# Order of the splits at two seams and width of the last product in a one-core decoder layer

## The chip, the cores and the metric

The kernel runs on one core of one Trainium2 chip. The metric is the device time of one execution in microseconds; lower is better.

## The reference

One layer of a decoder over 256 tokens of 1024 features, in float32: half a feed-forward network (SwiGLU, 2816 wide), a mixer (block attention of 8 heads beside a causal pooling mixer), cross-attention to 256 memory tokens, and half a feed-forward network again. Each sub-layer normalises its input, and normalises its output before it is added to the stream:

```python
def rmsnorm(x, g):
    r = lax.rsqrt(jnp.mean(x * x, axis=-1, keepdims=True) + RMS_EPS)
    return (x * r) * g

h = rmsnorm(x, ffn1_pre_g);  x = x + 0.5 * rmsnorm(swiglu(h, w_gate, w_up, w_down), ffn1_post_g)
h = rmsnorm(x, mix_pre_g);   x = x + rmsnorm(concat([attn(h), pool(h)]) @ w_out, mix_post_g)
h = rmsnorm(x, xa_pre_g);    x = x + rmsnorm(cross_attention(h, mem_n), xa_post_g)
h = rmsnorm(x, ffn2_pre_g);  x = x + 0.5 * rmsnorm(swiglu(h, ...), ffn2_post_g)
```

## The kernel before

Every product is made of three: each operand is split into a high part (rounded) and a low part (the rest), and low x high, high x high and high x low are added up. ACT makes a high part by a cast, DVE the low part by a subtraction. For the weights this is done by **units** of eight 128x128 tiles (1024 columns): `_make` casts the unit (L76) and subtracts (L77). `get` hands out tiles in the order in which TensorE uses them, and at the first tile of each unit it first makes all units up to so many units ahead. That number is taken from the list `pace`, one entry for each unit, and is `LEAD` = 4 where the list is empty. Making an even unit issues on SP the load (L66) of the pair of units that comes two units later; there are four buffers for pairs and seven for split units.

The 256 tokens are two tiles of 128. At the end of each sub-layer stands a **seam** (`row_end`). The last three units of its output product (`LATE` = 3) are multiplied row-wise: `row_sums` takes tile 0 and then tile 1 (L304 to L306), squares and sums on ACT (L332), scales on DVE (L335); `row_add` adds the result to the stream (L357). Then the stream is turned for the next sub-layer: `x_turn` transposes four chunks of 128 features on TensorE (L363), `x_hi` makes their high parts on ACT (L384), and `x_lo` their low parts on DVE (L388); both read the transposes in place, in PSUM.

Two seams have **fillers**: two half products of the cross-attention keys (one unit each), which keep TensorE busy meanwhile. There the order is: `products` (three units), `middle` (high and low parts of tile 0, `row_add` of tile 1), filler 0, `turned(0)` (chunks 0 to 3 of tile 1), filler 1, `turned(1)` (chunks 4 to 7 of tile 1). Behind it comes `group`, the first product of the next sub-layer: eight k steps of four tiles, thus four units. In each step L233 multiplies the four low weight parts by the high input, then L238 and L240 the four high parts by the high and the low input. `before` puts onto ACT the squares of the new stream (L532) and the flush of the fillers' result (L924, L925). The third seam has no fillers; it uses `early` and `late` in place of `turned`.

Within a seam (from `row_end` to the end of `group`) every engine takes its instructions in the order of the program. Outside, TensorE does, and a planner orders the others. Inside the region also stands the load of the next normalisation's gains on SP (`post_load`, L524), whose target is the buffer of the old ones.

The **tail** is `last_rows`: the last three units row-wise, and for each token tile the root, the scaled addition and the transfer out. For tile 1 the first 256 columns of the addition go over TensorE: identity times the stream (L736) plus a diagonal of the roots (made on ACT, L740) times the scaled rows (L741), copied by ACT (L745) and sent by ACT's queue (L748), while DVE does the other 768 columns (L753) and SP sends them (L746, L747).

Of the kernel before, what the change touches and what calls it, by code (L numbers as in the profile page):

```python
# [15 lines left out]
P = 128  # L16
D = 1024
S = 256
# [9 lines left out]
LEAD = 4  # L28
# [114 lines left out]
def build(nc, io, tiles_only=False):  # L143
    pr = Program()
    st = {}
# [7 lines left out]
    def tmp(shape, name, **kw):  # L153
        return st["tmp"].tile(shape, F32, name=name, **kw)

    def keep(shape, name):
        return st["keep"].tile(shape, F32, name=name)

    def xsplit():
        return st["xs"].tile([P, ND, 2 * S], F32R, name="xs")  # L160

    def gain(name, c):
        j = GAINS.index(name) * ND + c
        return st["gain"][:, j:j + 1]
# [179 lines left out]
    def row_root(sums, between=None):  # L344
        s, last = sums
        nc.scalar.activation(s[:, 5:6], s[:, last:last + 1], AF.Sqrt, bias=s[:, 4:5], scale=1.0 / D)
        if between:
            between()
        nc.vector.reciprocal(s[:, 6:7], s[:, 5:6])
        return s[:, 6:7]  # L350

    def quarter(i):
        return slice(i * S, (i + 1) * S)

    def row_add(t, d, r):
        x = st["xt"][:, t, d]
        nc.vector.scalar_tensor_tensor(x, st["ys"][:, t, d], r, x, op0=ALU.mult, op1=ALU.add)  # L357

    def x_turn(t, chunks, alloc):

        ps = alloc()
        for i, c in enumerate(chunks):
            nc.tensor.transpose(ps[:, i * P:(i + 1) * P], st["xt"][:, t, c * P:(c + 1) * P], st["ident"])  # L363
            st["turned", t, c] = ps[:, i * P:(i + 1) * P]
# [13 lines left out]
    def row_end(parts, ks, weights, factor, nxt, pre, fillers):  # L378


        box = {}

        def x_hi(t, c):
            nc.scalar.activation(st[nxt][:, c, t * P:(t + 1) * P], st["turned", t, c], AF.Copy, scale=gain(pre, c))  # L384

        def x_lo(t, c):
            X = st[nxt]
            nc.vector.scalar_tensor_tensor(X[:, c, S + t * P:S + (t + 1) * P], st["turned", t, c], gain(pre, c),  # L388
                                           X[:, c, t * P:(t + 1) * P].bitcast(F32), op0=ALU.mult, op1=ALU.subtract)

        def products():
            st["w"].pace = [(LEAD, None)] * (LATE - 1)
            st["w"].pace += [(LEAD - 1, None)] + [(LEAD - 2, None)] * 3 + [(LEAD - 1, None)] * 2 if fillers else []
            ws = [st["w"].get(UNIT) for _ in ks]
            st["w"].flush()
            st["ys"] = keep([P, 2, D], "y")
            r = row_root(row_sums(parts, ks, ws, 0, factor))
            st[nxt] = xsplit()
            st["xsum"] = tmp([P, 2, 2], "xsum")
            for d in HALVES:  # L400
                row_add(0, d, r)
            box["later"] = []
            between = {} if fillers else {(1, i): lambda i=i: turn_first(i) for i in range(2)}
            box["sums"] = row_sums(parts, ks, ws, 1, factor, box["later"], between)
            if fillers:
                for i in range(2):
                    x_turn(0, range(4 * i, 4 * i + 4), small)

        def turn_first(i):

            x_turn(0, range(4 * i, 4 * i + 4), small)
            if i == 0:
                for c in range(3):
                    x_hi(0, c)

        def middle():
            if fillers:
                r = row_root(box["sums"])
                for c in range(ND):
                    x_hi(0, c)  # L420
                for i in range(2):
                    row_add(1, quarter(i), r)
                box["later"][0]()
                for i in range(2, 4):
                    row_add(1, quarter(i), r)
                for c in range(ND):
                    x_lo(0, c)
                return
            for c in range(4):
                x_lo(0, c) if c < 3 else (x_hi(0, c), x_lo(0, c))  # L430
            box["r"] = row_root(box["sums"])

        def turned(i):
            def run():
                cs = range(4 * i, 4 * i + 4)
                x_turn(1, cs, accum)
                for c in cs:
                    x_hi(1, c)
                    x_lo(1, c)
            return run  # L440

        def before(j):
            if j == 1:
                k_flush()
            if j in (2, 4, 6, 7):
                rows_square(st["xt"], st["xsum"], {2: 0, 4: 1, 6: 2, 7: 3}[j])

        def early(k):

            r = box["r"]  # L450
            if k == 0:
                for c in range(4, ND):
                    x_hi(0, c)
                for i in range(2):
                    row_add(1, quarter(i), r)
                x_lo(0, 4)
                box["later"][0]()
                for c in range(5, ND):
                    x_lo(0, c)
                for i in range(2, 4):  # L460
                    row_add(1, quarter(i), r)
                for i in range(2):
                    rows_square(st["xt"], st["xsum"], i)
            if k == 6:
                x_turn(1, range(4), small)
                for c in range(4):
                    x_hi(1, c)
                for c in range(4):
                    x_lo(1, c)

        def late(k):

            if k == 0:
                x_turn(1, range(4, 8), small)
                for c in range(4, 8):
                    x_hi(1, c)
                for c in range(4, 8):
                    x_lo(1, c)
                for i in range(2, 4):
                    rows_square(st["xt"], st["xsum"], i)  # L480
            if k == 2:
                x_root()
            if k in (1, 3, 5):
                st["w"].ahead(k // 2 + 1)

        pr.add(products, weights)
        pr.add(middle)
        for i, f in enumerate(fillers):
            pr.add(*f)
            pr.add(turned(i))  # L490
        return before if fillers else (early, late)
# [36 lines left out]
    def rows_square(src, sums, i):  # L528

        t, half = divmod(i, 2)  # L530
        q = tmp([P, 512], "q")
        nc.scalar.activation(q, src[:, t, half * 512:(half + 1) * 512], AF.Square,  # L532
                             accum_out=sums[:, t, half:half + 1])
# [184 lines left out]
    def last_rows(parts, ks, weights):  # L718
        def run():
            ws = [st["w"].get(UNIT) for _ in ks]  # L720
            st["w"].flush()
            ys = st["ys"] = keep([P, 2, D], "y")
            xt = st["xt"]
            for t in range(2):
                o = io["out"][t * P:(t + 1) * P, :]
                later = [] if t else None
                s = row_sums(parts, ks, ws, t, 0.5, later)
                if t == 0:
                    r = row_root(s)
                    for i in range(4):  # L730
                        row_out(t, quarter(i), r)
                    for a, b in ((0, 512), (512, 1024)):
                        nc.sync.dma_start(o[:, a:b], ys[:, t, a:b])
                    continue
                turn = accum()
                nc.tensor.matmul(turn[:, :S], st["ident"], xt[:, t, quarter(0)], start=True, stop=False,  # L736
                                 skip_group_check=True)
                r = row_root(s, later[0])
                diag = tmp([P, P], "diag", bufs=1)
                nc.scalar.activation(diag, st["ident"], AF.Copy, scale=r)  # L740
                nc.tensor.matmul(turn[:, :S], diag, ys[:, t, quarter(0)], start=False, stop=True,  # L741
                                 skip_group_check=True)
                for d in (slice(512, 1024), quarter(1)):
                    row_out(t, d, r)
                nc.scalar.copy(ys[:, t, quarter(0)], turn[:, :S])  # L745
                nc.sync.dma_start(o[:, 512:], ys[:, t, 512:])  # L746
                nc.sync.dma_start(o[:, S:512], ys[:, t, S:512])  # L747
                nc.scalar.dma_start(o[:, :S], ys[:, t, :S])  # L748
        pr.add(run, weights)

    def row_out(t, d, r):
# [201 lines left out]
    def k_flush():  # L953
        while waiting:
            waiting.pop(0)()
# [270 lines left out]
```

## Time and profile before

| | us |
|---|---|
| median of 3 runs | 573.33 (573.03 to 573.44) |
| profiled execution | 573.43 |
| its span, first to last instruction | 571.6 |
| TensorE matmul busy | 562.0 (98%) |
| VectorE busy | 408.0 (71%) |
| ScalarE busy | 343.6 (60%) |

Busy times overlap; they are shares of the span and not additive. A time of the trace counts from the start of the span. A row of the view in order of time begins with the start and the length of an instruction, or of several alike that are merged; in brackets behind it stand the idle time of the engine before it and what ended that.

### The profile page before, as it was taken

What the parts mean: (1) busy time and instruction counts of PE and PEld (TensorE: products, weight loads), DVE (VectorE), ACT (ScalarE), POOL (GpSimd) and SP (SyncE); (2) the same over time, 40 slices, a digit from 0 to 9 for tenths busy, and PEclk for the clock granted to TensorE, in tenths of its full rate; (3) what the DMA queues carried; (4) which work ended last, traced back from release to release, by engine and by line L of the source; (5) the groups of instructions that cost most, each with busy time, mean ns of one, the idle gap of its engine ahead of it and who ended that gap; (6) DMA issues with size and microseconds to landing.
All of it is one profiled execution on the core that took longest, in us unless ns stands there. A gap on an engine that the chain in (4) does not pass through costs nothing.

```text
span 571.6 us, 8375 instructions
## 1 busy us (share of the span) xinstructions
PE 562.0 (98%) x3264; PEld 492.7 (86%) x3264; DVE 408.0 (71%) x661; ACT 343.6 (60%) x615; POOL 15.7 (3%) x34
## 2 busy tenths in 40 slices
PE   9999999999999999999999999999999999999996
PEld 8888888888888989988889988888888888888884
DVE  5989667777875678985478666466976776767644
ACT  7788665556556585884369456358754555555542
POOL 0000000000000000550000000000000000000000
PEclk9999999999999999999999999999999999999999
DMA  8996866555541378262077644332866556564102
GB/s 298 365 357 236 303 242 214 198 211 163 215 163 61 109 282 309 75 221 75 0 257 294 225 147 148 108 113 77 337 218 215 162 208 201 171 215 159 66 0 73
DMA packets 29255, 107.02 MB, mean 187 GB/s; under 512 B 2080, under 2 KB 2976, under 8 KB 28832
## 3 DMA queue, kind: packets, MB, share of 16 engines
q1 hardware_dynamic: 28640, 106.01, 52.3%
q10 hardware_dynamic: 576, 0.48, 0.3%
q8 instruction: 25, 0.41, 0.3%
q14 instruction: 14, 0.11, 0.1%
HBM read 105.44 MB, written 1.05 MB: 186 GB/s over the span
## 4 chain that ended last, share of the span: by engine, by line
PE 89%; DVE 6%; ACT 2%; DMA 2%; issue 1%; SPq 0%; DVEq 0%; ACTq 0%
PE sm L606 12%; PE acc L606 12%; PE acc L306 10%; PE acc L304 10%; PE acc L305 9%; PE acc L603 6%; PE sm L603 6%; PE acc L179 3%; PE acc L180 3%; PE acc L181 3%; DVE wlo L77 2%; PE acc L266 2%; PE acc L268 2%; PE acc L267 2%; DMA wraw<-w 2%; DVE xs L388 1%
## 5 line engine op out<-in xcount | busy, mean ns | idle before, releaser
L77 DVE TENSOR_TENSOR wlo<-wraw,whi 128x1024 fp32r<-128x1024 f32 x184 | 224.9, 1230 | 71.4 <-ACT whi L76 70.3
L76 ACT CAST whi<-wraw 128x1024 fp32r<-128x1024 f32 x184 | 191.7, 1052 | 48.6 <-PE acc L306 37.2
L606 PE MATMUL acc<-xs,whi 128*128 128x512 f32 x320 | 100.5, 395 | 0.0
L606 PE MATMUL sm<-xs,whi 128*128 128x512 f32 x320 | 100.5, 395 | 0.0
L603 PEld LDWEIGHTS acc<-xs,wlo 128*128 128x128 f32 x320 | 60.0, 188 | 14.5 <-DVE wlo L77 0.8
L603 PEld LDWEIGHTS sm<-xs,wlo 128*128 128x128 f32 x320 | 59.8, 188 | 13.8
L306 PE MATMUL acc<-whi,h 128*128 128x512 f32 x176 | 68.6, 390 | 0.2 <-DVE h L195 0.2
L304 PE MATMUL acc<-whi,h 128*128 128x512 f32 x176 | 68.6, 390 | 0.0
L305 PE MATMUL acc<-wlo,h 128*128 128x512 f32 x176 | 68.5, 389 | 0.0
L603 PE MATMUL acc<-xs,wlo 128*128 128x256 f32 x320 | 63.0, 278 | 0.6 <-DVE wlo L77 0.6
L603 PE MATMUL sm<-xs,wlo 128*128 128x256 f32 x320 | 63.2, 279 | 0.0
L606 PEld LDWEIGHTS sm<-xs,whi 128*128 128x128 f32 x320 | 48.7, 189 | 0.0
L606 PEld LDWEIGHTS acc<-xs,whi 128*128 128x128 f32 x320 | 48.7, 189 | 0.0
L179 PE MATMUL acc<-xs,wlo 128*128 128x256 f32 x160 | 46.1, 288 | 0.0
L180 PE MATMUL acc<-xs,whi 128*128 128x256 f32 x160 | 45.2, 283 | 0.0
L181 PE MATMUL acc<-xs,whi 128*128 128x256 f32 x160 | 45.2, 283 | 0.0
L611 ACT COPY cmb<-acc 128x256 f32<-128x256 f32 x40 | 14.9, 372 | 49.7 <-PE acc L606 49.7
L611 ACT COPY cmb<-sm 128x256 f32<-128x256 f32 x40 | 14.9, 372 | 49.2 <-PE sm L606 48.9
L306 PEld LDWEIGHTS acc<-whi,h 128*128 128x128 f32 x176 | 33.0, 188 | 7.7 <-DVE h L195 0.9
L305 PEld LDWEIGHTS acc<-wlo,h 128*128 128x128 f32 x176 | 33.0, 188 | 7.0
L304 PEld LDWEIGHTS acc<-whi,h 128*128 128x128 f32 x176 | 33.0, 188 | 7.0
L179 PEld LDWEIGHTS acc<-xs,wlo 128*128 128x128 f32 x160 | 30.6, 191 | 0.3
(196 smaller groups left out, 883.5 us busy)
## 6 DMA issues: line engine op xcount, KB each, us to landing
wraw<-w SPq DMA_DIRECT2D x91, 1024.0 KB, 4.9
post<-post SPq DMA_DIRECT2D x4, 512.0 KB, 5.2
wraw<-w SPq DMA_DIRECT2D x7, 256.0 KB, 5.7
wraw<-w SPq DMA_DIRECT2D x2, 512.0 KB, 7.1
y<-memt SPq DMA_DIRECT2D x1, 1024.0 KB, 5.2
y<-mem SPq DMA_DIRECT2D x1, 1024.0 KB, 7.0
xt<-xt SPq DMA_DIRECT2D x1, 1024.0 KB, 6.8
out_dram<-y SPq DMA_DIRECT2D x3, 256.0 KB, 2.1
```

The source lines that it names most:

```text
L76: self.nc.scalar.copy(hi, raw)
L77: eng.tensor_tensor(lo, raw, hi.bitcast(F32), op=ALU.subtract)
L179: nc.tensor.matmul(o, lo, X[:, :S], start=first, stop=False, skip_group_check=True)
L180: nc.tensor.matmul(o, hi, X[:, :S], start=False, stop=False, skip_group_check=True)
L181: nc.tensor.matmul(o, hi, X[:, S:], start=False, stop=last, skip_group_check=True)
L266: nc.tensor.matmul(box[t], a, hi, start=k == 0, stop=False)
L304: nc.tensor.matmul(o, a, hi, start=first, stop=False, skip_group_check=True)
L305: nc.tensor.matmul(o, a, lo, start=False, stop=False, skip_group_check=True)
L306: nc.tensor.matmul(o, b, hi, start=False, stop=last, skip_group_check=True)
L603: nc.tensor.matmul(ps[:, S:], lo, st[X][:, k + i, :S], start=k == i == 0, stop=False, skip_group_check=True)
L606: nc.tensor.matmul(ps, hi, st[X][:, k + i, :], start=False, stop=k + i == ND - 1, skip_group_check=True)
L611: nc.scalar.copy(c, ps[:, S:])
```

## The change

Three edits. At the two seams with fillers, `pace` gives 3 for the five units behind the first two, in place of 3, 2, 2, 2, 3, 3. In `turned` the four high parts of a half of tile 1 are issued before its four low parts; before, they alternated. In the tail TensorE's part of the addition is 128 columns wide in place of 256; DVE's second part is 384 wide in place of 256, and ACT's transfer stands ahead of SP's second one in the program.

```diff
         def products():
             st["w"].pace = [(LEAD, None)] * (LATE - 1)
-            st["w"].pace += [(LEAD - 1, None)] + [(LEAD - 2, None)] * 3 + [(LEAD - 1, None)] * 2 if fillers else []
+            if fillers:
+                st["w"].pace += [(LEAD - 1, None)] * 5
...
                 x_turn(1, cs, accum)
                 for c in cs:
                     x_hi(1, c)
+                for c in cs:
                     x_lo(1, c)
...
-                nc.tensor.matmul(turn[:, :S], st["ident"], xt[:, t, quarter(0)], start=True, stop=False,
+                nc.tensor.matmul(turn[:, :P], st["ident"], xt[:, t, :P], start=True, stop=False,
                                  skip_group_check=True)
                 r = row_root(s, later[0])
                 diag = tmp([P, P], "diag", bufs=1)
                 nc.scalar.activation(diag, st["ident"], AF.Copy, scale=r)
-                nc.tensor.matmul(turn[:, :S], diag, ys[:, t, quarter(0)], start=False, stop=True,
+                nc.tensor.matmul(turn[:, :P], diag, ys[:, t, :P], start=False, stop=True,
                                  skip_group_check=True)
-                for d in (slice(512, 1024), quarter(1)):
+                for d in (slice(512, 1024), slice(P, 512)):
                     row_out(t, d, r)
-                nc.scalar.copy(ys[:, t, quarter(0)], turn[:, :S])
+                nc.scalar.copy(ys[:, t, :P], turn[:, :P])
                 nc.sync.dma_start(o[:, 512:], ys[:, t, 512:])
-                nc.sync.dma_start(o[:, S:512], ys[:, t, S:512])
-                nc.scalar.dma_start(o[:, :S], ys[:, t, :S])
+                nc.scalar.dma_start(o[:, :P], ys[:, t, :P])
+                nc.sync.dma_start(o[:, P:512], ys[:, t, P:512])
```

## Rows read from the trace of the kernel before

**Rows 1.** The page's head.
```profile
span 571.6 us, 8375 instructions
```
**Rows 2.** What TensorE waited for: us in total, times, longest.
```profile
PE acc L233 <- DVE wlo L77: 2.6, 2, 1.3
```
**Rows 3.** TensorE in order of time: group of the first seam, then of the second.
```profile
199.33 0.28 PE L240 MATMUL acc<-xs,whi 128*128 128x256 f32 x1
...
201.63 0.74 PE L233 MATMUL acc<-xs,wlo 128*128 128x256 f32 x4
...
203.17 0.64 PE L233 MATMUL acc<-xs,wlo 128*128 128x256 f32 x4
...
206.06 0.75 PE L233 MATMUL acc<-xs,wlo 128*128 128x256 f32 x4 [1.29 <-DVE wlo L77]
...
207.59 0.64 PE L233 MATMUL acc<-xs,wlo 128*128 128x256 f32 x4
...
209.03 0.64 PE L233 MATMUL acc<-xs,wlo 128*128 128x256 f32 x4
...
296.61 0.64 PE L233 MATMUL acc<-xs,wlo 128*128 128x256 f32 x4
...
299.50 0.74 PE L233 MATMUL acc<-xs,wlo 128*128 128x256 f32 x4 [1.30 <-DVE wlo L77]
```
**Rows 4.** ACT in order of time, first seam.
```profile
192.35 2.16 ACT L384 ACTIVATE xs<-sm,gain 128x128 fp32r<-128x128 f32 x8
195.62 0.37 ACT L384 ACTIVATE xs<-acc,gain 128x128 fp32r<-128x128 f32 x1 [1.11 <-PE acc L363]
197.44 0.37 ACT L384 ACTIVATE xs<-acc,gain 128x128 fp32r<-128x128 f32 x1 [1.45 <-DVE xs L388]
...
199.28 1.04 ACT L76 CAST whi<-wraw 128x1024 fp32r<-128x1024 f32 x1
...
203.71 1.04 ACT L76 CAST whi<-wraw 128x1024 fp32r<-128x1024 f32 x1
```
**Rows 5.** DVE in order of time, first seam.
```profile
195.00 2.15 DVE L388 SCALAR_TENSOR_TENSOR xs<-sm,gain,xs 128x128 fp32r<-128x128 f32 x8
...
200.35 1.23 DVE L77 TENSOR_TENSOR wlo<-wraw,whi 128x1024 fp32r<-128x1024 f32 x1 [0.58 <-ACT whi L76]
...
204.78 1.23 DVE L77 TENSOR_TENSOR wlo<-wraw,whi 128x1024 fp32r<-128x1024 f32 x1 [0.58 <-ACT whi L76]
```
**Rows 6.** ACT in order of time, third seam: four high parts of tile 1.
```profile
385.40 1.14 ACT L384 ACTIVATE xs<-sm,gain 128x128 fp32r<-128x128 f32 x4 [1.17 <-PE sm L363]
```
**Rows 7.** SP's issues around the first seam; weight loads: count, size, median us to landing.
```profile
163.95 5.76 SPq L66 DMA_DIRECT2D wraw<-w  x2
194.19 0.34 SPq L524 DMA_DIRECT2D post<-post  x1
...
wraw<-w SPq DMA_DIRECT2D x91, 1024.0 KB, 4.9
```
**Rows 8.** All engines in order of time: the tail.
```profile
566.97 1.15 DVE L753 SCALAR_TENSOR_TENSOR y<-y,fs,xt 128x512 f32<-128x512 f32 x2
...
567.43 0.70 PE L741 MATMUL acc<-y,diag 128*128 128x256 f32 x2 [1.58 <-ACT diag L740]
...
568.16 0.37 ACT L745 COPY y<-acc 128x256 f32<-128x256 f32 x1 [0.79 <-PE acc L741]
568.19 0.37 SPq L747 DMA_DIRECT2D out_dram<-y  x1
568.57 0.35 ACTq L748 DMA_DIRECT2D out_dram<-y  x1
```
**Rows 9.** Transfers out: count, size, median us from issue to landing.
```profile
out_dram<-y SPq DMA_DIRECT2D x3, 256.0 KB, 2.1
...
out_dram<-y SPq DMA_DIRECT2D x1, 128.0 KB, 2.2
out_dram<-y ACTq DMA_DIRECT2D x1, 128.0 KB, 2.1
```

## The prediction

> **What bounds the kernel now.** I read the page's head first: the span is 571.6 us [rows 1], and the profiled execution took 573.43 us, so 1.8 us lie around the span. Of the three runs the median is 573.33, so this execution stands 0.10 us above it. TensorE is busy 98% of the span, so the next view is the list of what TensorE waited for. Its largest entry is the low-part product of the group (L233) waiting for a low half of a weight unit from DVE (L77): 2.6 us in two waits, one at each seam that has fillers [rows 2]. The next, 1.6 us, is in the tail, where the product with the diagonal waits for ACT [rows 8]. So TensorE's own order of work is the path, and the change can win what TensorE loses in these two waits and what it shortens behind the last product.
>
> Third view: TensorE in order of time through the first seam. Count weight units from u, the first of the three units of the seam's row products. Units u+3 and u+4 are the two fillers, u+5 to u+8 the group's eight k steps, two per unit. A k step that is not disturbed takes 209.03 - 207.59 = 1.44 us. The step that opens unit u+7 should follow the one at 203.17 at 204.61 and starts at 206.06: 1.45 us lost. It also takes 207.59 - 206.06 = 1.53, 0.09 more than the plain step. The step that opens u+6 takes 203.17 - 201.63 = 1.54, also 0.10 too long [rows 3]. At the second seam the same step comes 299.50 - 296.61 = 2.89 after its predecessor, again 1.45 too late [rows 3].
>
> Fourth: why so late? ACT and DVE in order of time. ACT has done the eight high parts of tile 0 at 194.51. Then it alternates with DVE: the high part at 195.62, and the next only at 197.44, after 1.45 us idle that DVE's low part ended [rows 4]. The casts of u+6 and u+7 stand in this queue at 199.28 and 203.71 [rows 4], and DVE's subtracts follow at 200.35 and 204.78, ending 201.58 and 206.01 [rows 5]. 206.01 is what TensorE's 206.06 waits for, and 201.58 is 0.05 before it opens u+6. So the queue of ACT and DVE inside the seam, not their total work and not DMA, sets both.
>
> **The change, part by part.**
>
> *Splits three units ahead.* From the pace lists: before, the row products split u+4 and u+5, filler 0 nothing, filler 1 u+6, and the group's units u+7; u+8 and u+9; u+10; u+11 and u+12. After: filler 0 splits u+6, filler 1 u+7, then u+8; u+9; u+10 and u+11; u+12. The number of splits is the same; u+6, u+7 and u+8 move one step forward. Each brings one cast (1.04 us) on ACT and one subtract (1.23 us) on DVE [rows 4, 5]. Where they land:
> - ACT, u+6: behind the eight high parts of tile 0, at 194.5, ready by 195.55. ACT sat idle there for 1.11 us until 195.62, when the transposes of tile 1 arrive [rows 4]. So it is free; if that cover were gone, it would cost up to 1.04 us to the high parts of tile 1.
> - DVE, u+6: behind the eight low parts of tile 0, which end at 197.15 [rows 5]. It runs from 197.1 to 198.3, and the first low part of tile 1 moves from there to about 198.3, done by 198.6. TensorE first reads it at 199.33 (L240) [rows 3]. 0.7 us are left; this is the thinnest cover of the change.
> - u+7: cast behind the four high parts, about 196.7 to 197.8, subtract behind the four low parts, about 199.4 to 200.6. TensorE opens u+7 at 204.6: 4 us to spare in place of 1.45 too late.
> - u+8: subtract done at about 203; needed at 207.5.
> - SP: a split of an even unit issues the load of the pair two ahead. u is odd at both seams (63 and 91 by counting tiles), so u+6 issues none, and u+7 issues the pair u+9, u+10 one place earlier, ahead of the load of the gains (L524). That load waits until 194.19 for the last use of the old gains; SP had been done with its last weight loads at 169.7 and stood there for 24 us [rows 7]. The pair's buffer is free long before, so its load moves to that idle time. What is queued behind it on SP is the load of the gains, which waits for DVE to 194.19 anyhow: no cost. The raw halves of u+6 to u+8 come from pairs issued by 169.7; a pair lands in 4.9 us at the median [rows 7], so they are there twenty microseconds early.
>
> *Four high parts together.* No instruction is added. Eight handovers between ACT and DVE per half become one. The third seam already runs this order: four high parts of tile 1 in 1.14 us [rows 6], against 3.66 us here from the first at 195.62 to the cast behind the fourth at 199.28 [rows 4]. The first half becomes ready about a microsecond sooner in spite of the subtract in front of it. By itself this takes the wait at u+7 away only in part; together with the splits it takes all. Both edits aim at the same loss, so it is counted once.
>
> *Worth at the seams.* Per seam 1.45 + 0.09 = 1.54 us, twice 3.1 us. The 0.10 at the opening of u+6 goes as well if it came from the subtract at 201.58: 0 to 0.2 for both, and I take 0.2, since the opening of u+7, which is known to have waited, shows the same surcharge. What is late next? After the group DVE and ACT are ahead of where they were by three to five microseconds, TensorE only by 1.6, so the covers grow. Sum: 3.3, bounds 2.9 to 3.4.
>
> *Tail.* The chain of the last tile goes through the product with the diagonal (L741, 0.70 us for two passes), the copy (L745, 0.37) and ACT's transfer, issued at 568.57 [rows 8]. With 128 of 256 columns the product and the copy cost between half and all of that: a gain of 0 to 0.53 us; taking a little over half of it, 0.3, ACT's transfer starts at 568.25 and, at 2.1 us [rows 9], lands at 570.35 in place of 570.67. But SP's second transfer now waits for a 384-column DVE step in place of a 256-column one. The two steps of 768 columns take 1.15 us [rows 8]; in proportion 128 more cost 0.19, at the least nothing; I take 0.13. It is then issued at 568.32 in place of 568.19 [rows 8] and lands 2.2 later [rows 9], at 570.52. This becomes the last. What follows the last landing up to the span's end, 0.9 us, stays. Gain 570.67 - 570.52 = 0.15; I count 0.1, bounds -0.1 to 0.3. The half more bytes in it I count at nothing: 256 KB landed in 2.1 and 128 KB in 2.2 [rows 9]. The Trainium skill speaks against this (DMA: Bandwidth & Descriptors, "Anatomy of one DMA"): a transfer there costs a fixed 2.0 us and then its bytes at 436 GB/s, fitted for another issuing path. By it 64 KB more would cost an estimated 0.15 us, which would leave no gain in the tail and 570.1 as the sum; the rows of this trace show no such slope.
>
> Sum against the profiled execution: 573.43 - 3.3 - 0.1 = 570.0. Against the median it would be 569.9; I stay at 570.0, since a small new wait is likelier than a gain I have not seen.
>
> **Rivals.**
> 1. *The wait moves to the low parts of tile 1.* If DVE puts them later than I have them (0.7 us of cover), TensorE waits at the first k step instead. With both splits in front of them, the first low part would be done at about 199.9 in place of 198.6, 0.5 us late per seam. The gain shrinks to 2 x (1.64 - 0.5) + 0.1 = 2.4: 571.0. With the edge at a full 1.2 us it is 572.4. For it: DVE gets more work ahead of these parts. Against it: inside the seam the order is the program's, and only u+6 stands before the first half.
> 2. *It doesn't do what it says.* If the late subtract were set by a load or by a buffer and not by the queue, putting the split earlier would leave the wait where it is; only the tail would move, 573.3. Against it: ACT stands idle between high parts with DVE as the releaser, and DVE's idle time before the two subtracts is ended by the cast [rows 5].
> 3. *Slower: ACT blocks on a raw unit.* ACT takes its queue in order, so the high parts of tile 1 now stand behind the cast of u+6. If that unit's load came behind the load of the gains, it would be issued at about 194.6 and land at 199.5; the cast would end at 200.5, the subtract at 201.8, the first low part at 202.2, 2.8 us after TensorE's 199.33. Less the 1.64 won that is 1.2 worse per seam, 575.7 in all. It decides once the unit lands later than about 198.3. Against it: the counting above; an odd u puts u+6 into a pair issued before the seam.
> 4. *Planner.* Outside the seams ACT and DVE are ordered by a planner, whose choice may shift; TensorE shows no wait there now, so I count some tenths either way, inside the forecast's own range.
>
> **How the numbers follow.** Forecast 0.80 (569.5 to 570.7, from the seams' 2.9 to 3.4, the tail's bounds and some tenths of rival 4); rival 1 0.10 (571.0, to 572.2 at the most); rival 2 0.06 (573.3); rival 3 0.04 (575.7). The range 569.5 to 571.4 takes the forecast and most of rival 1. 0.2% is 1.15 us, about what a measurement of this kernel can tell from no change: faster means under 572.2. Forecast and rival 1 give 0.90, rival 2 0.06, rival 3 0.04.
>
> **What would show it.** In the profile after: the list of TensorE's waits has no L233 behind L77; the eight k steps take 11.6 us in place of 13.3; ACT shows four high parts of tile 1 in one row of some 1.1 us, with the cast of u+6 before them and of u+7 behind; DVE has the subtract of u+6 between the low parts of the two tiles; SP shows one more weight load before the gains. In the tail ACT's transfer is issued before SP's second one. I would be wrong if TensorE waits for a low part (L240 behind L388) or if a wait of similar size turns up in the stretch behind the group.

## The result and the profile after

| | us |
|---|---|
| kernel before, median of 4 runs | 573.38 (573.03 to 573.98) |
| changed kernel, median of 4 runs | 569.97 (569.73 to 570.26) |
| ratio | 0.994 (95% interval 0.9922 to 0.9957) |
| profiled execution of the changed kernel | 570.26, span 568.4 |

The change makes the kernel 3.4 us faster, 0.6%, and the time is the one forecast (570.0). By the stages of the trace 3.35 us of it come from the two seams; the tail, to which the forecast gave 0.1, is 0.06 shorter, which the time of a run cannot tell from nothing.

What TensorE waited for in the changed kernel (us in total, times, longest). The row of [rows 2] is gone; the rest are the tail (1.8) and the opening of the kernel (at 1.18, 6.41 and 18.67 us of the span). The tail's wait is 0.2 longer than before because the product ahead of it has become that much shorter. Line numbers behind the pace list are one or two higher than before.

```profile
PE acc L743 <- ACT diag L742: 1.8, 1, 1.8
PE warm L509 <- DVE cmb L506: 1.2, 1, 1.2
PE acc L238 <- ACT whi L108: 0.6, 1, 0.6
PE acc L605 <- DVE wlo L77: 0.3, 1, 0.3
```

TensorE of the changed kernel in order of time, the group of the first seam (start, length), to be laid beside [rows 3]:

```profile
198.95 0.72 PE L233 MATMUL acc<-xs,wlo 128*128 128x256 f32 x4
...
199.62 0.28 PE L240 MATMUL acc<-xs,whi 128*128 128x256 f32 x1
...
201.90 0.64 PE L233 MATMUL acc<-xs,wlo 128*128 128x256 f32 x4
...
204.78 0.64 PE L233 MATMUL acc<-xs,wlo 128*128 128x256 f32 x4
...
210.54 0.28 PE L179 MATMUL acc<-xs,wlo 128*128 128x256 f32 x1
```

Every step behind the first takes 1.44 us, those that open u+6 (201.90) and u+7 (204.78) too. The eight steps end at 210.54, 11.59 us after their start. ACT and DVE in the same stretch, for [rows 4, 5]:

```profile
192.65 2.17 ACT L384 ACTIVATE xs<-sm,gain 128x128 fp32r<-128x128 f32 x8
194.65 1.10 ACT L76 CAST whi<-wraw 128x1024 fp32r<-128x1024 f32 x1
195.91 1.15 ACT L384 ACTIVATE xs<-acc,gain 128x128 fp32r<-128x128 f32 x4 [0.16 <-PE acc L363]
196.93 1.06 ACT L76 CAST whi<-wraw 128x1024 fp32r<-128x1024 f32 x1
...
195.29 2.16 DVE L388 SCALAR_TENSOR_TENSOR xs<-sm,gain,xs 128x128 fp32r<-128x128 f32 x8
197.36 1.21 DVE L77 TENSOR_TENSOR wlo<-wraw,whi 128x1024 fp32r<-128x1024 f32 x1
198.50 1.12 DVE L388 SCALAR_TENSOR_TENSOR xs<-acc,gain,xs 128x128 fp32r<-128x128 f32 x4
199.53 1.21 DVE L77 TENSOR_TENSOR wlo<-wraw,whi 128x1024 fp32r<-128x1024 f32 x1
```

The cast of u+6 lies in ACT's former idle time (0.16 us of 1.11 are left), its subtract between the low parts of the two tiles, and the subtract of u+7 ends at 200.74, 4.04 us before TensorE opens the unit. On SP three weight loads, not two, now precede the gains [rows 7]:

```profile
164.26 10.95 SPq L66 DMA_DIRECT2D wraw<-w  x3
```

The opening of the kernel differs by some tenths from one execution to the next, once by over a microsecond, so times since the start mislead by that much. A ruler that is free of it: the first transposes (L363) of the three seams. Of the kernel before, then of the changed one:

```profile
191.24 1.03 PE L363 MATMUL sm<-const,xt 128*128 128x128 f32 x8
284.67 1.04 PE L363 MATMUL sm<-const,xt 128*128 128x128 f32 x8
378.38 0.60 PE L363 MATMUL sm<-const,xt 128*128 128x128 f32 x4
```

```profile
191.53 1.03 PE L363 MATMUL sm<-const,xt 128*128 128x128 f32 x8
283.30 1.04 PE L363 MATMUL sm<-const,xt 128*128 128x128 f32 x8
375.32 0.60 PE L363 MATMUL sm<-const,xt 128*128 128x128 f32 x4
```

From the first seam to the second 93.43 became 91.77, from the second to the third 93.71 became 92.02: 1.66 and 1.69 us, 3.35 together. The opening was 0.29 later in this execution, by chance: the same code stands there.

### The profile page after: what moved, and what is told of

The parts are those of the page before. It is cut to its first block, busy times and chain, and to the rows that moved or that the text cites. A ratio compares the mean times of both kernels' runs of the same rounds, so it can differ in the third digit from the quotient of the medians.

```text
span 568.4 us, 8389 instructions
## 1 busy us (share of the span) xinstructions
PE 560.8 (99%) x3264; PEld 492.4 (87%) x3264; DVE 407.2 (72%) x661; ACT 342.3 (60%) x615; POOL 15.7 (3%) x34
## 4 chain that ended last, share of the span: by engine, by line
PE 94%; DVE 2%; ACT 1%; DMA 1%; issue 1%; SPq 0%; DVEq 0%; ACTq 0%
PE acc L608 13%; PE sm L608 12%; PE acc L306 10%; PE acc L304 10%; PE acc L305 10%; PE acc L605 6%; PE sm L605 6%; PE acc L179 3%; PE acc L180 3%; PE acc L181 3%; PE acc L268 2%; PE acc L267 2%; PE acc L266 2%; PE acc L233 1%; PE acc L238 1%; PE acc L240 1%
## 5 line engine op out<-in xcount | busy, mean ns | idle before, releaser
L306 PE MATMUL acc<-whi,h 128*128 128x512 f32 x176 | 68.6, 390 | 0.1
L306 PEld LDWEIGHTS acc<-whi,h 128*128 128x128 f32 x176 | 33.0, 188 | 7.6 <-DVE h L195 0.8
```

The costliest lines, as they stand in the source:

```text
L306: nc.tensor.matmul(o, b, hi, start=False, stop=last, skip_group_check=True)
```

## The experiments

All use one ruler: first seam to second, and second to third, as above, beside the time. Each ratio is to executions of the kernel before that were taken beside the run. The four runs on the tail's transfers are one execution each and stand further down.

| kernel | median us | ratio to before (95%) | seam 1 to 2 | seam 2 to 3 |
|---|---|---|---|---|
| before | 573.38 | | 93.43 | 93.71 |
| changed | 569.97 | 0.994 (0.9922 to 0.9957) | 91.77 | 92.02 |
| pace alone | 569.98 | 0.9941 (0.9929 to 0.9954) | 91.77 | 92.02 |
| high parts together alone | 569.92 | 0.994 (0.9927 to 0.9952) | 91.79 | 92.02 |
| tail alone | 573.37 | 1.0 (0.9992 to 1.0009) | 93.45 | 93.71 |
| both splits first | 570.87 | 0.9956 (0.9942 to 0.9969) | 92.27 | 92.52 |
| splits late | 571.78 | 0.9972 (0.9961 to 0.9982) | 92.68 | 92.93 |

**The pace alone.** The kernel before with

```diff
-            st["w"].pace += [(LEAD - 1, None)] + [(LEAD - 2, None)] * 3 + [(LEAD - 1, None)] * 2 if fillers else []
+            if fillers:
+                st["w"].pace += [(LEAD - 1, None)] * 5
```

> The kernel before with the new pace list alone (splits three units ahead at the two seams with fillers; high and low parts of tile 1 still alternate; old tail). Theory Q, the queue of ACT and DVE worked forward in the times of the first seam of the kernel before: u+6 is cast at 194.5, subtract done 198.4; u+7 cast at about 200.5, subtract done 202.8, needed at 204.6; u+8 subtract done 207.2, needed at 207.5. So no wait of TensorE is left and the whole of the seams' gain is there: 570.1. Rival S, as the prediction's sentence on the two edits has it: the edits share the gain, each alone wins only a part; then this one gives about 571 to 572, and TensorE still waits for a low half of a unit (L233 behind L77) at u+8.

Measured: 569.98, and no wait of L233. Theory Q holds and S falls. The group's queue in this kernel, ACT and DVE, and TensorE's opening of u+8:

```profile
198.44 0.37 ACT L384 ACTIVATE xs<-acc,gain 128x128 fp32r<-128x128 f32 x1 [2.59 <-DVE xs L388]
199.23 0.37 ACT L384 ACTIVATE xs<-acc,gain 128x128 fp32r<-128x128 f32 x1 [0.42 <-DVE xs L388]
...
201.35 1.23 DVE L77 TENSOR_TENSOR wlo<-wraw,whi 128x1024 fp32r<-128x1024 f32 x1 [0.58 <-ACT whi L76]
...
205.78 1.23 DVE L77 TENSOR_TENSOR wlo<-wraw,whi 128x1024 fp32r<-128x1024 f32 x1 [0.58 <-ACT whi L76]
...
207.24 0.64 PE L233 MATMUL acc<-xs,wlo 128*128 128x256 f32 x4
```

The alternation is still there, and the waits of ACT have even grown (2.59 us behind the subtract of u+6). They cost nothing, since u+7 is ready at 202.58 and u+8 at 207.01, 0.23 us before TensorE opens it.

**The high parts together alone.** The kernel before with

```diff
                 for c in cs:
                     x_hi(1, c)
+                for c in cs:
                     x_lo(1, c)
```

> The kernel before with four high parts ahead of four low parts alone (old pace, old tail). Theory Q: the high parts of the first half end at 196.7, u+6 cast 196.7 to 197.7 and subtract done 199.4; second half of the low parts done 201.2; u+7 subtract done 202.4, needed at 204.6: no wait left, 570.1. Rival S, the prediction's own words (by itself it takes the wait away only in part): 571 to 572, with a shorter wait of L233 behind L77.

Measured: 569.92, the whole gain again. DVE in this kernel:

```profile
196.86 1.11 DVE L388 SCALAR_TENSOR_TENSOR xs<-acc,gain,xs 128x128 fp32r<-128x128 f32 x4
197.90 1.21 DVE L77 TENSOR_TENSOR wlo<-wraw,whi 128x1024 fp32r<-128x1024 f32 x1
199.90 1.13 DVE L388 SCALAR_TENSOR_TENSOR xs<-acc,gain,xs 128x128 fp32r<-128x128 f32 x4 [0.79 <-ACT xs L384]
200.94 1.21 DVE L77 TENSOR_TENSOR wlo<-wraw,whi 128x1024 fp32r<-128x1024 f32 x1
```

With the old pace u+6 is ready at 199.11 and u+7 at 202.15; TensorE opens them at 201.39 and 204.27:

```profile
201.39 0.64 PE L233 MATMUL acc<-xs,wlo 128*128 128x256 f32 x4
...
204.27 0.64 PE L233 MATMUL acc<-xs,wlo 128*128 128x256 f32 x4
```

So the two edits are not parts of a sum. Each alone takes away all of the wait, and the second one to come is worth nothing in time; what it adds is spare time (4.04 us at u+7 with both, 2.12 with the high parts together alone; 0.23 at u+8 with the pace alone).

**The tail alone.** The kernel before with the last hunk of the change.

> The kernel before with the new tail alone (TensorE's part 128 columns wide). Both theories: 573.2 to 573.3, not to be told from no change by the time. By the trace: from the start of the last product of the row-wise stage (L306) to the last landing 5.65 us in the kernel before; the prediction has 5.5 (SP's second transfer last). Rival: ACT's transfer of 512 bytes a row lands later than one of 1024 bytes a row (2.4 against 2.1 us, as the one profile of the changed kernel has it), then ACT's transfer stays the last and the figure is 5.6 or more.

Measured: 573.37 against 573.34 for the kernel before beside it, no difference. The rival's landing time is there: ACT's transfer 2.4 us. More on it below.

**Both splits first.** The changed kernel with

```diff
-                st["w"].pace += [(LEAD - 1, None)] * 5
+                st["w"].pace += [(LEAD - 1, None), (LEAD, None)] + [(LEAD - 1, None)] * 3
```

> The changed kernel with both splits, u+6 and u+7, put in front of the first half of tile 1 (pace 4 at filler 0). This prices the cover of 0.7 us that the prediction calls the thinnest. Theory Q: the first low part of tile 1 is done at 199.7 in place of 198.6 (times of the first seam of the kernel before) and TensorE, which wants it at 199.33, waits 0.4 us plus 0.1 of restart at the first k step (L240 behind L388) at each seam: 571.0. Rival: if the cover is wider than the trace's own times say, nothing is lost: 570.0.

Measured: 570.87, 0.90 above the changed kernel, and 0.50 more at each seam. DVE, then TensorE at the first step:

```profile
196.95 2.35 DVE L77 TENSOR_TENSOR wlo<-wraw,whi 128x1024 fp32r<-128x1024 f32 x2
199.22 2.15 DVE L388 SCALAR_TENSOR_TENSOR xs<-acc,gain,xs 128x128 fp32r<-128x128 f32 x8
...
199.62 0.39 PE L240 MATMUL acc<-xs,whi 128*128 128x256 f32 x1 [0.24 <-DVE xs L388]
```

This is the first rival of the prediction, made to happen, at its price. It also shows that an earlier split is not free: one unit in front of the low parts fits into their cover, two do not. The row says 0.24 us of idle time, the step is 0.51 longer (198.53 to 200.55 against 1.51 in the changed kernel). Counted from the seam's first transposes (191.11 here, 191.53 there) the product starts 0.42 later, and behind it the step loses the other 0.09. The busy time that the trace gives the product before a wait thus hides part of it, so a lost time is read from the starts of equal steps.

**Splits late.** The changed kernel with

```diff
-                st["w"].pace += [(LEAD - 1, None)] * 5
+                st["w"].pace += [(n, None) for n in (3, 2, 1, 2, 3, 3)]
```

> The changed kernel with the pace lowered so far that neither filler splits anything and u+6 and u+7 are both split at the group's first step (pace 3, 2, 1, 2, 3, 3 behind the first two). Theory Q, in times of the first seam of the kernel before: both casts stand behind the second four high parts (200.0 to 202.0 on ACT), the subtract of u+6 behind the second four low parts, done at 202.3; TensorE wants it at 201.6 and opens u+6 0.75 late, plus 0.1 of restart; the subtract of u+7 is done at 203.6 and in time. So one wait of L233 behind L77 at each seam, moved from u+7 to u+6, and 0.85 us per seam: 571.7. Rival: if what counts is only that high parts come four together, nothing is lost: 570.0.

Measured: 571.78; 0.91 more at each seam. TensorE waits where it was foreseen, at the opening of u+6 and not of u+7 (the step before, the late one, the one behind; then the list of waits):

```profile
201.56 0.64 PE L233 MATMUL acc<-xs,wlo 128*128 128x256 f32 x4
...
203.82 0.74 PE L233 MATMUL acc<-xs,wlo 128*128 128x256 f32 x4 [0.66 <-DVE wlo L77]
...
205.35 0.64 PE L233 MATMUL acc<-xs,wlo 128*128 128x256 f32 x4
...
PE acc L233 <- DVE wlo L77: 1.3, 2, 0.7
```

It opens 0.82 late, and the step takes 0.09 more than the plain one. So a loss at a seam can be set to 0, 0.5, 0.9 or 1.7 us by the order of the same instructions alone. The 1.7 was read from the trace before; the other three had been worked out from the queue by hand (0, 0.5 and 0.85) before those kernels ran.

**The tail's transfers.** Three questions were open: why ACT's transfer lands 0.3 later after its issue than it did, whether its rows of 512 bytes are to blame, and what sets the end of the tail. Each kernel stands on one profile here, and the runs without a transfer leave a piece of the output out.

TensorE's part 192 columns wide, in the changed kernel (the identity product, the copy and DVE's part follow):

```diff
...
-                nc.tensor.matmul(turn[:, :P], diag, ys[:, t, :P], start=False, stop=True,
+                nc.tensor.matmul(turn[:, :192], diag, ys[:, t, :192], start=False, stop=True,
...
-                nc.scalar.dma_start(o[:, :P], ys[:, t, :P])
-                nc.sync.dma_start(o[:, P:512], ys[:, t, P:512])
+                nc.scalar.dma_start(o[:, :192], ys[:, t, :192])
+                nc.sync.dma_start(o[:, 192:512], ys[:, t, 192:512])
```

> The changed kernel with TensorE's part of the tail 192 columns wide (768 bytes a row), for its rows. Counted from the start of the last row-wise product (L306): in the changed kernel ACT's transfer is issued 3.22 and SP's second one 3.26 later, in the kernel before (256 columns) 3.55 and 3.17. Here ACT's at 3.4 and SP's at 3.2. If the landing time of ACT's transfer goes with the length of a row, it is 2.4 us at 512 bytes, 2.1 to 2.2 at 1024, and between here, about 2.2 to 2.3; the last landing is then 5.6 to 5.7 after that product, as in both kernels. If it goes with ACT's transfer being issued together with SP's, it is 2.1 to 2.2 here.

The queues exchanged, in the changed kernel:

```diff
-                nc.scalar.dma_start(o[:, :P], ys[:, t, :P])
-                nc.sync.dma_start(o[:, P:512], ys[:, t, P:512])
+                nc.sync.dma_start(o[:, :P], ys[:, t, :P])
+                nc.scalar.dma_start(o[:, P:512], ys[:, t, P:512])
```

> The changed kernel with the two last transfers exchanged between the queues: SP sends TensorE's 128 columns, ACT the 384 columns of DVE. If the 2.4 us to landing belong to rows of 512 bytes, SP's last transfer now shows 2.4 and ACT's about 2.2; if they belong to ACT's queue, ACT's shows 2.4 and SP's 2.2. The time: 570.0, a tenth either way.

Without SP's second transfer:

```diff
-                nc.sync.dma_start(o[:, P:512], ys[:, t, P:512])
```

> The changed kernel without SP's second transfer of the tail: columns 128 to 511 of the second token tile are not sent, so this piece of the output is left out; all else stays. ACT's 64 KB then have no transfer issued beside them. In the changed kernel they land 2.4 us after their issue, in the kernel before (128 KB, issued 0.38 behind SP's) 2.1, at 192 columns (0.19 behind) 2.3, and with the queues exchanged ACT's 192 KB took 2.4 and SP's 64 KB 1.9. Theory C, it shares the way with SP's transfer issued at the same moment: 1.9 to 2.1 here, last landing 5.1 to 5.3 after the start of the last row-wise product. Theory A, ACT's queue itself takes 2.4 for this transfer: 2.4 again, 5.6 after.

Without SP's first transfer:

```diff
-                nc.sync.dma_start(o[:, 512:], ys[:, t, 512:])
```

> The changed kernel without SP's first transfer of the tail: columns 512 to 1023 of the second token tile are not sent, so this piece of the output is left out; all else stays. ACT's 64 KB and SP's 192 KB are still issued 0.04 us apart. Theory C1, ACT's transfer waits on its way for all bytes issued before it: with half of them gone it lands after 2.1 to 2.2. Theory C2, only the transfer issued at the same moment matters: 2.4 again.

The transfers out by queue and size (count, size, median us from issue to landing): the changed kernel, then the exchange, then without SP's second, then without SP's first transfer.

```profile
out_dram<-y SPq DMA_DIRECT2D x1, 192.0 KB, 2.2
out_dram<-y ACTq DMA_DIRECT2D x1, 64.0 KB, 2.4
```

```profile
out_dram<-y ACTq DMA_DIRECT2D x1, 192.0 KB, 2.4
out_dram<-y SPq DMA_DIRECT2D x1, 64.0 KB, 1.9
```

```profile
out_dram<-y ACTq DMA_DIRECT2D x1, 64.0 KB, 1.8
```

```profile
out_dram<-y SPq DMA_DIRECT2D x1, 192.0 KB, 2.0
out_dram<-y ACTq DMA_DIRECT2D x1, 64.0 KB, 2.2
```

At 192 columns ACT's 96 KB took 2.3. That 2.3 is what the length of a row would give, so this run alone would have pointed the wrong way. Rows of 512 bytes are not to blame: SP sends them in 1.9 with both other transfers in flight, and ACT in 1.8 where SP's second transfer is missing. By that same 1.8 ACT's queue is not slow by itself either. What ACT's transfer takes alone was not run: without SP's second transfer SP's first is still under way, issued 0.50 us ahead:

```profile
564.24 0.33 SPq L748 DMA_DIRECT2D out_dram<-y  x1
564.74 0.35 ACTq L749 DMA_DIRECT2D out_dram<-y  x1
```

So SP's second transfer, issued within 0.04 us of ACT's, makes most of the difference: 1.8 became 2.4. That is theory C, though the 1.8 is a tenth below the range it gave. SP's first seems to add the rest: without it ACT's took 2.2 and SP's second 2.0 in place of 2.2, as C1 has it and not C2. This rests on one profile, in which SP's issue stood 0.02 us ahead of ACT's and not behind. Of two transfers issued within 0.04 us ACT's landed later whichever was the larger (64 KB in 2.4 against 192 KB in 2.2; exchanged, 192 KB in 2.4 against 64 KB in 1.9). Which piece of the way is shared was not tried.

The kept traces hold the landings finer than these views show them. By them the last landing, always ACT's, comes 5.69 us after the start of the last row-wise product (L306) in the kernel before, 5.63 in the changed one, 5.65 with 192 columns, 5.63 with the queues exchanged, 5.43 without SP's first transfer and 5.00 without its second. The times were 569.88 us with 192 columns, 570.19 with the queues exchanged (a tenth more than expected, in one execution), 569.67 and 569.22 without SP's first and second. So the end of the tail hardly depends on which part comes first or how wide it is.

## Why the prediction was right

*The bound.* TensorE's order was the path, and its two waits for a low half of a unit were the loss. That the wait went to nothing and the time went down by the length of the stalls shows it; the tail's edit, alone, moved no time that can be told from noise.

*The size.* The prediction counted 1.45 + 0.09 per seam and 0.10 for the opening of u+6, 1.64; measured 1.66 and 1.69. The doubtful 0.10 was real: the opening of u+6 now takes 1.44 in place of 1.54. That the total came out to 0.03 us is in part luck: the seams gave 0.05 more than forecast and the tail a little less. It was right not to take the 2.6 us of the list of waits for the loss, but the distance between starts of equal steps.

*The cover.* The first low part was to be done by 198.6, with 0.7 us to spare. Measured, in an execution that opened 0.29 later, it starts at 198.50 and is done at about 198.84 (0.34 for a single one, as in the kernel before); TensorE reads at 199.62. That the cover was as thin as said is shown by both splits first, which overran it by 0.5. (At the most that rival costs 572.4 by the terms of its own paragraph, not the 572.2 that stands among the chances.) One sentence beside it was mis-sized: the first half was to be ready about a microsecond sooner. Its last low part ended at 199.76 before and at 199.62 in the changed kernel, so 0.4 sooner with the later opening taken off; the prediction's own times (199.4 against 199.76) give the same.

*Nothing late next.* The prediction had DVE and ACT three to five microseconds ahead behind the group. The sums of the squares, DVE's reduction for the next root, of the kernel before and of the changed one:

```profile
213.16 0.15 DVE L279 TENSOR_REDUCE rs<-xsum 128x2 f32<-128x4 f32 x1
```

```profile
208.59 0.15 DVE L279 TENSOR_REDUCE rs<-xsum 128x2 f32<-128x4 f32 x1
```

4.6 us earlier, with an opening that was 0.29 later, where TensorE gained 1.66. The planner's stretches gave nothing back: the third seam's start moved by the whole sum.

*Wrong: what each edit is worth.* "By itself this takes the wait at u+7 away only in part; together with the splits it takes all." Each takes all. The sentence was written without working the queue forward for that edit alone, as had been done for both together; done afterwards, ahead of the run, it gave 202.4 for u+7 against 204.6 needed. The total was not touched, since the loss was counted once. A reason why ACT waits for DVE's read at all stands in the Trainium skill (PSUM — Partial Sum Buffer, "PSUM bank collisions raise a hardware error": two engines must be kept apart on one bank, reads included). The trace agrees in that ACT waits 0.42 us for DVE between high parts of chunks that share one PSUM tile; no run here shows what would come without the wait. But what the alternation cost was ACT's time, and that became TensorE's loss only because the casts stood behind it.

*Wrong: the tail.* Of its terms the product (0.70 to 0.49), the copy (0.37 to 0.27) and DVE's 0.13 came as estimated (that ACT's transfer would start at 568.25 should have read 568.27, on which nothing hung); the rows of the changed kernel, for [rows 8]:

```profile
561.89 0.40 PE L306 MATMUL acc<-whi,h 128*128 128x512 f32 x1
...
563.84 1.28 DVE L755 SCALAR_TENSOR_TENSOR y<-y,fs,xt 128x512 f32<-128x512 f32 x2
...
564.29 0.49 PE L743 MATMUL acc<-y,diag 128*128 128x128 f32 x2 [1.79 <-ACT diag L742]
...
564.82 0.27 ACT L747 COPY y<-acc 128x128 f32<-128x128 f32 x1 [0.58 <-PE acc L743]
565.11 0.38 ACTq L749 DMA_DIRECT2D out_dram<-y  x1
565.15 0.33 SPq L750 DMA_DIRECT2D out_dram<-y  x1
```

In the kernel before the last row-wise product stood at 565.02:

```profile
565.02 0.40 PE L306 MATMUL acc<-whi,h 128*128 128x512 f32 x1
```

ACT's issue thus moved from 3.55 to 3.22 us behind that product. The term that failed is the landing time, carried over from [rows 9] as if it belonged to the transfer. It went from 2.15 to 2.40, since the transfer is now issued within 0.04 us of SP's second one, where before it came 0.38 behind; by the finer times it is issued 0.32 sooner and lands 0.06 sooner. For the same reason SP's second transfer, which the prediction had as the last, is not: it landed 5.45 behind the product, ACT's 5.63. So the tail's gain is near the forecast 0.1 by luck. The sum by the Trainium skill's rule (DMA: Bandwidth & Descriptors, "Anatomy of one DMA"), no gain in the tail, is as near, and not by its mechanism either: SP's 192 KB landed in the same 2.2 us as 128 KB before.

*Left open.* The third rival, ACT blocked by a raw unit that has not landed, was not tried: the load of the gains could not be put ahead of the unit's load without also changing which buffers it waits for. In the changed kernel it did not happen: the cast of u+6 stands at 194.65 directly behind the high parts of tile 0, with no idle time before it. The second falls with the runs that change the order alone.

## What to carry to other kernels

Where one engine is the path and another feeds it in program order, write the feeding engine's queue out with durations from the trace and compare each item's end with the moment it is wanted; here this gave the loss at a seam to within 0.1 us for four orders that had not been run. Work it out for each edit alone too: two edits that speed the same queue may each be enough. And a transfer's time to landing belongs to what is in flight with it, so issuing the last one sooner need not land it sooner.

## What the runs showed of the hardware

A transfer of 64 KB out on ACT's queue landed after 1.8 us with 256 KB on SP's queue issued 0.50 us before it, after 2.2 with 192 KB on SP's queue issued at the same moment, and after 2.4 to 2.5 with both. In the nine profiles that send all of the output, before and changed kernel included, the last landing came 5.63 to 5.71 us after the start of the last row-wise product, though the last issue moved from 3.55 to 3.26 behind it. A step of TensorE's group that opened behind a late operand took 0.09 to 0.10 us more than the plain 1.44, beside the time by which it opened late.
